# A two-layer decoder trunk: loads taken in turn, a written order for the first projection, and squares of the norm on ScalarE

## The chip, the cores and the metric

One core of one Trainium2 chip runs the whole kernel. The metric is the device time of one execution in microseconds; the time of a version is the median over its runs. The engines are TensorE (PE), VectorE (DVE), ScalarE (ACT), GpSimd (POOL) and SyncE (SP, which only issues loads and stores here).

## The reference

The input x has 512 tokens of 1024 channels, float32. Two layers follow one another, and each adds a mixer and a gated feed-forward part to x:

```
for layer in range(2):
    h = rms_norm(x, norm_mix[layer])
    x = x + (even_mixer(h, ...) if layer == 0 else odd_mixer(h, ...))
    h = rms_norm(x, norm_ffn[layer])
    x = x + (silu(h @ w_gate) * (h @ w_up)) @ w_down        # 1024 -> 2816 -> 1024
rms_norm(x, g) = x * rsqrt(mean(x * x, -1) + 1e-6) * g
```

The mixer of layer 0 is stick-breaking attention (8 heads of 64) beside a gated convolution over three tokens (512 channels), from one input projection and into one output projection. The mixer of layer 1 picks, for each query, the 128 keys with the largest score of a small indexer, and does softmax attention over them (16 query heads, 4 key heads, norms on queries and keys, a bias that depends on distance).

## The kernel before, in words

The residual x lives transposed on the chip, as eight chunks of 128 channels by 512 tokens (`xT`). A float32 product is made of three products in a rounded format: each operand is split into a high half (ScalarE: `wh`, `hr`) and a low half (VectorE: `wl`, `lr`, the operand less its high half), and `mm3` (L104 to L106) adds high by high, high by low and low by high into one PSUM bank. A product of 128 by 512 stands for one of these three. A weight tile is loaded by SP into one of three raw buffers (`raw`, L146) and split into one of three pairs (`wh` L149, `wl` L150); a tile is needed every eight slots. A slot is one call of `slot()`, made after each three products: `after(n, f)` runs f n slots later, and so sets where f's instructions stand in the order that is traced. Where the text says slot n, it counts from the end of a projection.

Outside of `manual_schedule` a scheduler orders each engine's instructions by its own model; inside it, TensorE, VectorE, ScalarE and GpSimd follow the order that was traced. Before the change this covers only the mixer of layer 1 (up to the start of its feed-forward part).

The head. x comes in token-major and is turned into chunks by TensorE with the identity (L382), two chunks per load; ScalarE makes the high half times the norm's gain (L174) and a kept copy of the chunk (L385), VectorE the low half (L175). The turns go through two `z` banks. The rsqrt of the norm isn't applied to h but to results: the query products start on x times gain. They go into four banks (L104 to L106), and `first_rstd` makes the tokens' sums of squares on VectorE (L396), the rsqrt on ScalarE and a Newton step, and spreads the result over the partitions with `dg` (L409) and a product with ones (L411) into `rbc`. `stack` empties the four banks (copies L420, low halves L424), and the key products, again L104 to L106, take the first bank that comes free. Ahead of it all stand 24 warm-up products of ones (L331, two instructions each).

The norms behind a projection. `residual_proj` adds each result of a projection to `xT` (L657, or L654 and L655 where rbc scales it), splits the new chunk (L174, L175) for the next projection, and adds its square into `ssq`: GpSimd squares and adds (L268, L272, L273), and for the last chunk ScalarE squares (L275) and VectorE adds (L276). `rstd_mm` runs some slots into the next projection (6 behind layer 0's mixer and layer 1's mixer, 7 behind layer 0's feed-forward part): the product with ones (L289), L291, a table load and rsqrt on ScalarE (L292), three Newton instructions (L281 to L283). Eight slots later `rstd_cols` (L300, L302) makes the same values one per token. The evacuations of the next projection wait for rbc.

Of the kernel before, what the change touches and what calls it, by code (L numbers as in the profile page):

```python
# [8 lines left out]
F32 = mybir.dt.float32  # L9
F32R = mybir.dt.float32r  # L10
ALU = mybir.AluOpType
AF = mybir.ActivationFunctionType
# [3 lines left out]
P = 128  # L16
S = 512
D = 1024
# [3 lines left out]
HC = HID // P  # L22
WARM = 24
ORDER = None
RATE0, LAG0 = 0.8, 5
LAGR_FFN, LAGR_MIX = 5, 7
L1_ORDER = {mybir.EngineType.PE, mybir.EngineType.DVE, mybir.EngineType.Activation,
            mybir.EngineType.Pool}
LAG_W, LAG_KI, LAG_DOT, LAG_CH, LAG_TK, LAG_TQ, LAG_T1, LAG_N, LAG_C, LAG_LO, LAG_P, EXPS = 3, 8, 5, 4, 8, 6, 4, 8, 11, 2, 3, 1
LAG_Z = 14  # L30
# [10 lines left out]
TAKEN = -3.4e38  # L41
ARENA_KB = 104.5

EARLY = 2
# [9 lines left out]
LAG_TK = 8  # L54
LAGR_FFN = 6
LAG_KLO = 1
# [19 lines left out]
class Net:  # L76
# [65 lines left out]

    def new_weights(self, src, kk, n, lo):
        nc = self.nc
        raw = self.wraw.tile([P, kk, n], F32, name="raw", tag="raw")
        nc.sync.dma_start(raw, src)  # L146
        wh = self.wsp.tile([P, kk, n], F32R, name="wh", tag="wh")
        wl = self.wsp.tile([P, kk, n], F32R, name="wl", tag="wl")
        nc.scalar.copy(wh, raw)  # L149
        (lo or nc.vector).tensor_tensor(wl, raw, wh.bitcast(F32), op=ALU.subtract)  # L150
        return wh, wl
# [111 lines left out]

    def stats_add(self, c):

        nc = self.nc
        if c == 0:
            nc.gpsimd.tensor_tensor(self.ssq, self.xT[:, c], self.xT[:, c], op=ALU.mult)  # L268
            return
        sq = self.cst.tile([P, S], F32, name="sqx", tag="sqx")  # L270
        if c < KC - 1:
            nc.gpsimd.tensor_tensor(sq, self.xT[:, c], self.xT[:, c], op=ALU.mult)  # L272
            nc.gpsimd.tensor_tensor(self.ssq, self.ssq, sq, op=ALU.add)  # L273
        else:
            nc.scalar.activation(sq, self.xT[:, c], AF.Square)  # L275
            nc.vector.tensor_tensor(self.ssq, self.ssq, sq, op=ALU.add)  # L276

# [6 lines left out]

    def rstd_mm(self):

        nc = self.nc
        ps = self.bank("z", "pstat")
        nc.tensor.matmul(ps, self.ones, self.ssq, start=True, stop=True)  # L289
        v = self.cst.tile([P, S], F32, name="sqx", tag="sqx")  # L290
        nc.vector.tensor_scalar(v, ps, 1.0 / D, EPS, op0=ALU.mult, op1=ALU.add)  # L291
        nc.scalar.activation(self.rbc, v, AF.Abs_reciprocal_sqrt)  # L292
        self.newton(self.rbc, v, self.ssq)
        self.after(8, self.rstd_cols)

# [9 lines left out]
    def setup(self):  # L305
# [20 lines left out]
        self.cols = cst.tile([P, 48], F32, name="cols")  # L326
        nc.scalar.dma_start(rows, I["norm_mix"].rearrange("l (c p) -> (l c) p", p=P))

        warm = self.bank("z", "pstat")
# [6 lines left out]
    def setup_rest(self):  # L336
        nc, I = self.nc, self.I
        rows = self.rows2
        nc.scalar.dma_start(rows[0:16, :], I["norm_ffn"].rearrange("l (c p) -> (l c) p", p=P))
        nc.scalar.dma_start(rows[16:28, :], I["ev_conv_w"][0].rearrange("w (c p) -> (w c) p", p=P))  # L340
# [30 lines left out]

    def load_x(self, xp):

        nc = self.nc
        xr = self.I["x"].rearrange("o (b p) d -> p (o b) d", p=P)
        xt = xp.tile([P, TB, D], F32, name="x_tm")
        for i in range(4):
            nc.sync.dma_start(xt[:, :, i * 256:(i + 1) * 256], xr[:, :, i * 256:(i + 1) * 256])
            for c in (2 * i, 2 * i + 1):
                ps = self.bank("z", "pstat")  # L380
                for tb in range(TB):
                    nc.tensor.transpose(ps[:, tb * P:(tb + 1) * P], xt[:, tb, c * P:(c + 1) * P],  # L382
                                        self.ident)
                self.split(self.xh3(c), ps, g=self.g_mix(0, c))
                nc.scalar.copy(self.xT[:, c], ps)  # L385
            self.x_tm = xt
            yield

    def first_rstd(self, xp):
# [14 lines left out]
        nc.vector.tensor_scalar(self.rq[:, TB:], self.rcol, 0.125, None, op0=ALU.mult)  # L404
        dg = xp.tile([P, S], F32, name="dg")
        ps = self.bank("z", "pstat")
        for tb in range(TB):
            t = slice(tb * P, (tb + 1) * P)
            nc.vector.tensor_scalar(dg[:, t], self.ident, self.rcol[:, tb:tb + 1], None,  # L409
                                    op0=ALU.mult)  # L410
            nc.tensor.matmul(ps[:, t], self.ones, dg[:, t], start=True, stop=True)  # L411
# [121 lines left out]
    def layer0_mix(self):  # L533
# [8 lines left out]
        with self.tc.tile_pool(name="xin", bufs=1) as xp:  # L542

            loads = self.load_x(xp)
            ps = [self.acc() for _ in range(4)]
            next(loads)
            for k0 in range(0, KC, 2):
                next(loads, None)
                wh, wl = self.weights(W[k0 * P:(k0 + 2) * P, 0:512].rearrange(
                    "(k p) n -> p k n", p=P), 2, 512)  # L550
                for m in range(4):
                    c = slice(m * P, (m + 1) * P)
                    for k in range(2):
                        h, l = xs[k0 + k]
                        self.mm3(ps[m], wh[:, k, c], wl[:, k, c], h, l, k0 + k == 0,
                                 k0 + k == KC - 1)
            self.first_rstd(xp)
            for m in range(4):
                qs = self.R(32 + 4 * m, 2, S)
                self.stack([(qs[0][:, e], qs[1][:, e]) for e in range(2)], ps[m])  # L560
                heads.append(qs[0])
        self.setup_rest()
# [6 lines left out]
        with self.tc.tile_pool(name="l0", bufs=1) as sp:  # L569
# [67 lines left out]
            for j in range(4):  # L637
# [5 lines left out]
            self.residual_proj(I["ev_w_out"][0], att + conv, self.xh3,  # L643
                               lambda c: self.g_ffn(0, c), pair=2)

    def residual_proj(self, W, ins, out3, gain, scale_r=False, tmp=None, pair=1, part=False,
                      lo=None):

        nc = self.nc

        def ev(m, ps):
# [4 lines left out]
            else:  # L656
                nc.vector.tensor_tensor(self.xT[:, m], self.xT[:, m], ps, op=ALU.add)  # L657
            if not part:
                self.split(out3(m), self.xT[:, m], g=gain(m))
                self.stats_add(m)  # L660
        self.proj_fm(W, 0, D, ins, ev, pair=pair, lo=lo)
        if not part:
            self.after(LAGR_MIX if scale_r else LAGR_FFN, self.rstd_mm)


    def ffn(self, layer, xs, g0):
# [5 lines left out]
        with self.tc.tile_pool(name=f"ffn{layer}", bufs=2) as fp:  # L672
# [30 lines left out]
            if not last:  # L703
                self.plan(self.fm_tiles(Wd, 0, D, HC, 256, 4, 1, None) + self.l1_tiles())
                self.residual_proj(Wd, gs, self.xh3, lambda c: self.g_mix(1, c), scale_r=True,
                                   tmp=fp)
                return
# [23 lines left out]
    def layer1_mix(self):  # L731
# [15 lines left out]
        with ExitStack() as es:  # L747
# [328 lines left out]
            while self.slots < start + 4 * len(order) + LAG_C + LAG_P + 4:  # L1076
                self.slot()
            self.few_banks(None)
            self.residual_proj(Wo[512:1024], half[4:8], lambda c: out3[c],
                               lambda c: self.g_ffn(1, c))  # L1080
        self.ffn(1, [(o[0], o[2]) for o in out3], 0)
# [49 lines left out]
```

## Time and profile before

| what | value |
|---|---|
| median of 3 runs | 1233.53 us (1232.91 to 1233.72) |
| the profiled execution | 1230.06 us |
| its span, first to last instruction | 1228.3 us |
| mean granted clock of TensorE | 0.996 |
| busy: TensorE, VectorE, ScalarE, GpSimd | 97%, 55%, 38%, 15% |

The profiled execution is one of its own, 3.47 us under the median; its span leaves out 1.76 us around the first and the last instruction. Matmuls overlap, so a busy TensorE is read from the distance of starts and not from durations.

### The profile page before, as it was taken

The page shows a single profiled execution, that of the slowest core. Times are in us where ns is not written, and L with a number is a line of the kernel's source. Part 1 is how long each engine was busy: PE and PEld are TensorE (multiplying, and loading weights), DVE is VectorE, ACT ScalarE, POOL GpSimd, SP SyncE. Part 2 cuts the span into 40 slices and gives each one's busy share as a digit, 9 for nine tenths or more (in the row PEclk, how much of TensorE's full clock was granted, in tenths as well). Part 3 has the DMA queues.
Part 4 walks back from the last instruction along what each step waited for, and adds up shares of the span by engine and source line. Part 5 has one row for each costly group of instructions (what it writes and reads, how often), then busy time and mean ns, then how long its engine had stood idle before and what let it go on. Part 6 is the DMA issues. An engine that isn't in the chain of part 4 may idle for free.

```text
span 1228.3 us, 14473 instructions
## 1 busy us (share of the span) xinstructions
PE 1196.7 (97%) x5573; PEld 982.4 (80%) x5573; DVE 669.5 (55%) x1064; ACT 466.2 (38%) x755; POOL 189.3 (15%) x228
## 2 busy tenths in 40 slices
PE   9999999999999999999999889998999999999998
PEld 8787878788888888888787678887888888888886
DVE  6769965634343343444589988757444444342322
ACT  5656733332233222222263379654322222322120
POOL 1334303200000000122135444226000000000000
PEclk9999999999999999999999999999999999999999
DMA  6231223333333332232223221112333233323330
GB/s 206 68 91 53 60 79 97 92 94 95 103 86 103 92 97 94 95 95 87 86 89 93 77 70 35 53 50 88 86 88 101 87 103 86 103 90 99 111 112 35
DMA packets 103637, 108.32 MB, mean 88 GB/s; under 512 B 4660, under 2 KB 89696, under 8 KB 103568
## 3 DMA queue, kind: packets, MB, share of 16 engines
q1 hardware_dynamic: 102768, 106.21, 29.0%
q10 hardware_dynamic: 800, 1.18, 0.3%
q8 instruction: 44, 0.72, 0.2%
q14 instruction: 25, 0.20, 0.1%
HBM read 105.24 MB, written 2.14 MB: 87 GB/s over the span
## 4 chain that ended last, share of the span: by engine, by line
PE 79%; DVE 12%; issue 5%; ACT 2%; POOL 2%; DMA 1%; ACTq 0%; POOLq 0%; DVEq 0%
PE acc L104 20%; PE acc L106 20%; PE acc L105 20%; PE acc L220 4%; PE acc L219 4%; PE acc L221 4%; DVE wl L150 2%; DVE w L825 1%; DVE L L828 1%; PE pt L1009 1%; DVE arena L175 1%; DVE om L458 1%; DVE xT L657 1%; PE z L433 1%; PE po L105 1%
## 5 line engine op out<-in xcount | busy, mean ns | idle before, releaser
L104 PE MATMUL acc<-arena,wh 128*128 128x512 f32 (+2 forms) x1176 | 468.1, 398 | 1.4 <-DVE xT L657 1.0
L106 PE MATMUL acc<-arena,wl 128*128 128x512 f32 (+2 forms) x1176 | 459.8, 391 | 0.0
L105 PE MATMUL acc<-arena,wh 128*128 128x512 f32 (+2 forms) x1176 | 456.7, 388 | 1.4 <-DVE arena L175 1.3
L150 DVE TENSOR_TENSOR wl<-raw,wh 128x1024 fp32r<-128x1024 f32 (+1 forms) x175 | 220.8, 1262 | 347.3 <-ACT wh L149 347.2
L149 ACT CAST wh<-raw 128x1024 fp32r<-128x1024 f32 (+1 forms) x191 | 198.6, 1041 | 462.7 <-issue 196.5
L106 PEld LDWEIGHTS acc<-arena,wl 128*128 128x128 f32 (+1 forms) x1176 | 220.7, 188 | 50.3 <-issue 0.2
L105 PEld LDWEIGHTS acc<-arena,wh 128*128 128x128 f32 (+1 forms) x1176 | 221.1, 188 | 47.4 <-DVE arena L175 2.3
L104 PEld LDWEIGHTS acc<-arena,wh 128*128 128x128 f32 (+1 forms) x1176 | 221.1, 188 | 45.1 <-DVE xT L657 2.1
L219 PE MATMUL acc<-wh,arena 128*128 128x512 f32 x272 | 108.9, 400 | 0.3 <-DVE arena L175 0.3
L220 PE MATMUL acc<-wl,arena 128*128 128x512 f32 x272 | 108.2, 398 | 0.0
L221 PE MATMUL acc<-wh,arena 128*128 128x512 f32 x272 | 108.1, 397 | 0.0
L221 PEld LDWEIGHTS acc<-wh,arena 128*128 128x128 f32 x272 | 51.4, 189 | 12.2
L219 PEld LDWEIGHTS acc<-wh,arena 128*128 128x128 f32 x272 | 51.5, 189 | 12.1 <-DVE arena L175 0.7
L220 PEld LDWEIGHTS acc<-wl,arena 128*128 128x128 f32 x272 | 51.5, 189 | 11.5
L683 DVE TENSOR_TENSOR ft<-acc,rbc 128x512 f32<-128x512 f32 x44 | 30.5, 692 | 55.2 <-PE acc L106 55.0
L268 POOL TENSOR_TENSOR ssq<-xT 128x512 f32<-128x512 f32 x3 | 3.5, 1169 | 327.8 <-DVE xT L655 274.0
L150 POOL TENSOR_TENSOR wl<-raw,wh 128x1024 fp32r<-128x1024 f32 x16 | 38.9, 2430 | 69.3 <-ACT wh L149 67.8
L685 ACT ACTIVATE fs<-ft 128x512 f32<-128x512 f32 x44 | 27.5, 629 | 52.2 <-DVE ft L683 52.2
L690 DVE TENSOR_TENSOR fp<-acc,fs 128x512 f32<-128x512 f32 x44 | 30.4, 692 | 28.5 <-PE acc L106 28.5
L433 PE MATMUL z<-arena 128*128 128x384 f32 (+3 forms) x120 | 41.2, 346 | 4.8 <-DVE mx L976 2.8
L976 DVE CUSTOM_DVE_ANT_0 L<-z,bias 128x128 f32<-128x128 f32 (+3 forms) x64 | 30.7, 486 | 18.2 <-PE z L975 17.6
L986 ACT ACTIVATE L<-L,mx 128x128 f32<-128x128 f32 (+3 forms) x64 | 35.8, 560 | 11.9 <-DVE sm L993 9.4
(205 smaller groups left out, 1285.9 us busy)
## 6 DMA issues: line engine op xcount, KB each, us to landing
raw<-in_ffn_w_gate_dram SPq DMA_DIRECT2D x44, 512.0 KB, 3.8
raw<-in_ffn_w_up_dram SPq DMA_DIRECT2D x44, 512.0 KB, 3.7
raw<-in_ffn_w_down_dram SPq DMA_DIRECT2D x42, 512.0 KB, 3.7
raw<-in_ev_w_in_dram SPq DMA_DIRECT2D x24, 512.0 KB, 3.9
raw<-in_od_w_in_dram SPq DMA_DIRECT2D x16, 512.0 KB, 3.5
raw<-in_ev_w_out_dram SPq DMA_DIRECT2D x8, 512.0 KB, 3.4
bias<-F SPq DMA_DIRECT2D x16, 256.0 KB, 3.2
raw<-in_od_w_out_dram SPq DMA_DIRECT2D x8, 512.0 KB, 3.4
```

The costliest lines, as they stand in the source:

```text
L104: mm(ps, wh, xh, start=first, stop=False)
L105: mm(ps, wh, xl, start=False, stop=False)
L106: mm(ps, wl, xh, start=False, stop=last)
L149: nc.scalar.copy(wh, raw)
L150: (lo or nc.vector).tensor_tensor(wl, raw, wh.bitcast(F32), op=ALU.subtract)
L219: mm(ps[tb], h[:, t], wh[:, k], start=c == 0, stop=False)
L220: mm(ps[tb], h[:, t], wl[:, k], start=False, stop=False)
L221: mm(ps[tb], l[:, t], wh[:, k], start=False, stop=c == kc - 1)
L433: self.nc.tensor.matmul(z, qs, kd, start=True, stop=False)
L683: nc.vector.tensor_tensor(t, ps, self.rbc, op=ALU.mult)
L976: nc.vector.tensor_tensor_reduce(out=u["ls"][:, r], in0=z, in1=bias[h][:, 0:nk][:, ::-1], scale=1.0, scalar=FILL, op0=ALU.add, op1=ALU.max ...
L986: nc.scalar.activation(ls[:, r], ls[:, r], AF.Exp, bias=mx[:, r:r + 1], accum_out=sm[:, r:r + 1])
```

## The change

Five things are changed.

1. x is loaded in five spans (128, 128, 256, 256 and 256 channels), and each of the first three is followed by the load of the query weights of the same channels. The products of the query go through these spans, under `manual_schedule`: the turns and splits of two chunks stand in the order ahead of the products of the chunks before them, and the kept copies right behind. 15 warm-up products are left, and a small ScalarE activation early in the setup draws its table load forward.
2. The token norms stay in that fixed order: the four reductions come behind the last weight split, then the stacks, then the product with ones.
3. The small loads of `setup_rest` wait, through a copy of `rcol`, until the token norms are there.
4. All squares behind a projection are made by ScalarE, into two buffers in turn where rbc isn't in use; GpSimd keeps the sum for all but the last chunk. Where rbc doesn't scale the result, the last chunk's square and sum come before its split.
5. The sums matmul comes at slot 8, 9 and 11 in place of 6, 7 and 6 (after the mixer of layer 0, after its feed-forward part, after the mixer of layer 1); behind the mixer of layer 0 there is no `rstd_cols`. The indexer's key in layer 1 is emptied two slots later.

```diff
-WARM = 24
+WARM = 15
-LAGR_FFN, LAGR_MIX = 5, 7
+LAGR_FFN, LAGR_MIX = 5, 9
-LAG_W, LAG_KI, ... = 3, 8, ...
+LAG_W, LAG_KI, ... = 3, 10, ...
+X_SPANS = ((0, 1), (1, 2), (2, 4), (4, 6), (6, 8))
-LAGR_FFN = 6
+LAGR_FFN = 8
...
-    def stats_add(self, c):
+    def stats_add(self, c, free):
         if c == 0:
-            nc.gpsimd.tensor_tensor(self.ssq, self.xT[:, c], self.xT[:, c], op=ALU.mult)
+            nc.scalar.activation(self.ssq, self.xT[:, c], AF.Square)
             return
-        sq = self.cst.tile([P, S], F32, name="sqx", tag="sqx")
-        if c < KC - 1:
-            nc.gpsimd.tensor_tensor(sq, self.xT[:, c], self.xT[:, c], op=ALU.mult)
-            nc.gpsimd.tensor_tensor(self.ssq, self.ssq, sq, op=ALU.add)
-        else:
-            nc.scalar.activation(sq, self.xT[:, c], AF.Square)
-            nc.vector.tensor_tensor(self.ssq, self.ssq, sq, op=ALU.add)
+        sq = (self.rbc if free and c % 2 else
+              self.cst.tile([P, S], F32, name="sqx", tag="sqx"))
+        nc.scalar.activation(sq, self.xT[:, c], AF.Square)
+        (nc.gpsimd if c < KC - 1 else nc.vector).tensor_tensor(self.ssq, self.ssq, sq, op=ALU.add)
...
-        self.after(8, self.rstd_cols)
+        if cols:
+            self.after(8, self.rstd_cols)
...
+        nc.scalar.activation(self.rcol[:, 0:1], self.zero, AF.Copy, scale=self.ones[:, 0:1])
...
+        nc.vector.tensor_copy(rows, self.rcol[0:32, 0:1].to_broadcast([32, P]))
         nc.scalar.dma_start(rows[0:16, :], I["norm_ffn"].rearrange("l (c p) -> (l c) p", p=P))
...
+    def load_x(self, xp, W):
+        xr = self.I["x"].rearrange("o (b p) d -> p (o b) d", p=P)
+        self.x_tm = xp.tile([P, TB, D], F32, name="x_tm")
+        raws = []
+        for i, (a, b) in enumerate(X_SPANS):
+            c = slice(a * P, b * P)
+            nc.sync.dma_start(self.x_tm[:, :, c], xr[:, :, c])
+            if i < 3:
+                raws.append(self.load_raw(W[c, 0:512].rearrange("(k p) n -> p k n", p=P),
+                                          b - a, 512))
+        return raws
+
+    def turn_x(self, c):
+        ps = self.bank("z", "pstat")
+        for tb in range(TB):
+            nc.tensor.transpose(ps[:, tb * P:(tb + 1) * P],
+                                self.x_tm[:, tb, c * P:(c + 1) * P], self.ident)
+        self.split(self.xh3(c), ps, g=self.g_mix(0, c))
+        return lambda: nc.scalar.copy(self.xT[:, c], ps)
+
+    def queries(self, W, raws):
...
+        keep = self.turn_x(0)
+        halves(0)
+        keep1 = self.turn_x(1)
+        keep()
+        halves(1)
+        keep1()
+        for i in range(5):
+            dot(i, (0, 1))
+            n = 2 + 2 * i
+            if n < KC:
+                keep = self.turn_x(n)
+            dot(i, (2, 3))
+            if n < KC:
+                keep1 = self.turn_x(n + 1)
+                keep()
+                halves(i + 2)
+                keep1()
...
+            raws = self.load_x(xp, W)
+            with self.tc.manual_schedule(engines=L1_ORDER):
+                self.queries(W, raws)
+                dg = self.first_rstd(xp)
                 for m in range(4):
-                qs = self.R(32 + 4 * m, 2, S)
-                self.stack([(qs[0][:, e], qs[1][:, e]) for e in range(2)], ps[m])
-                heads.append(qs[0])
+                    qs = self.R(32 + 4 * m, 2, S)
+                    self.stack([(qs[0][:, e], qs[1][:, e]) for e in range(2)], self.qps[m])
+                    heads.append(qs[0])
+                self.first_rbc(dg)
...
             if not part:
+                first = m == KC - 1 and not scale_r
+                if first:
+                    self.stats_add(m, not scale_r)
                 self.split(out3(m), self.xT[:, m], g=gain(m))
-                self.stats_add(m)
+                if not first:
+                    self.stats_add(m, not scale_r)
         self.proj_fm(W, 0, D, ins, ev, pair=pair, lo=lo)
         if not part:
-            self.after(LAGR_MIX if scale_r else LAGR_FFN, self.rstd_mm)
+            self.after(lagr, lambda: self.rstd_mm(cols))
```

Here `halves(i)` splits the weights of span i and `dot(i, ms)` makes its products into the banks ms. `lagr` is 8 by default and for layer 0's mixer, which also has `cols=False`; it is `LAGR_MIX` (9) behind layer 0's feed-forward part and 11 behind the mixer of layer 1.

## Rows read from the trace of the kernel before

**Rows 1.** The page, part 1: busy us, share of the span, instructions.

```profile
PE 1196.7 (97%) x5573; PEld 982.4 (80%) x5573; DVE 669.5 (55%) x1064; ACT 466.2 (38%) x755; POOL 189.3 (15%) x228
```

**Rows 2.** Windows, a quiet stretch: length, busy us (instructions) by engine, clock, DMA.

```profile
175.00:200.00 25.00, 25.00 (x111) 20.52 (x110) 11.51 (x13) 6.47 (x7) 0.00 (x0) 1.00 0.27 87
```

**Rows 3.** Waits of TensorE over the span: total us, times, longest.

```profile
PE pstat L289 <- DVE ssq L276: 4.7, 3, 3.7
```

**Rows 4.** Timeline of TensorE, head: start, us, operation, idle before it.

```profile
9.24 1.09 PE L382 MATMUL pstat<-eye,x_tm 128*128 128x128 f32 x8
...
10.67 0.51 PE L104 MATMUL acc<-arena,wh 128*128 128x512 f32 x1 [0.34 <-ACT arena L174]
...
36.46 1.05 PE L411 MATMUL pstat<-dg,ones 128*128 128x128 f32 x8
...
37.61 0.50 PE L104 MATMUL acc<-arena,wh 128*128 128x512 f32 x1
```

**Rows 5.** Windows of TensorE alone over the warm-up: busy, clock, DMA.

```profile
1.12:5.12 4.00, 4.00 (x19) 1.00 0.79 247
...
6.12:9.08 2.96, 2.96 (x28) 1.00 0.89 304
```

**Rows 6.** Chain that ended last, head: the turn of two chunks.

```profile
24.75 0.87 PE pstat L382 x8
```

**Rows 7.** Groups by line and tile: durations in ns (min/median/max), or busy us, mean ns.

```profile
L174 ACT ACTIVATE arena<-pstat,cols 128x512 fp32r<-128x512 f32 x8 | 5.2, 684 | 0.3 <-PE pstat L382 0.3
...
L385 ACT COPY xT<-pstat 128x512 f32<-128x512 f32 x8 | 4.5, 585 | 1.2 <-DVE arena L175 1.1
...
L149 ACT CAST wh<-raw x191: 622/1054/1082, 9.0 to 1207.5; 128x1024 fp32r<-128x1024 f32 x186, 128x512 fp32r<-128x512 f32 x4, 128x576 fp32r<-128x576 f32 x1
L150 DVE TENSOR_TENSOR wl<-raw,wh x175: 692/1226/2316, 10.0 to 1208.6; 128x1024 fp32r<-128x1024 f32 x170, 128x512 fp32r<-128x512 f32 x4, 128x576 fp32r<-128x576 f32 x1
...
L396 DVE CUSTOM_DVE_ANT_0 junk<-x_tm x4: 1215/1218/1227, 14.0 to 23.0; 128x1024 f32<-128x1024 f32 x4
```

**Rows 8.** Line L175, low halves of x, by source: ns min/median/max.

```profile
L175 DVE SCALAR_TENSOR_TENSOR arena<-xT,cols,arena x24: 740/1482/1782, 201.9 to 856.5; 128x512 fp32r<-128x512 f32 x24
L175 DVE SCALAR_TENSOR_TENSOR arena<-pstat,cols,arena x8: 740/745/750, 11.2 to 27.5; 128x512 fp32r<-128x512 f32 x8
```

**Rows 9.** Timeline of VectorE, head.

```profile
28.36 0.16 DVE L281 TENSOR_TENSOR t<-rcol 128x4 f32<-128x4 f32 x1
...
29.10 0.87 DVE L409 TENSOR_SCALAR dg<-eye,rcol 128x128 f32<-128x128 f32 x4
...
33.74 4.22 DVE L424 TENSOR_TENSOR arena<-acc,arena 64x512 fp32r<-64x512 f32 x6 [0.45 <-ACT arena L420]
```

**Rows 10.** Timeline of ScalarE, head: the first weight cast.

```profile
8.95 1.05 ACT L149 CAST wh<-raw 128x1024 fp32r<-128x1024 f32 x1 [3.78 <-DMA raw<-in_ev_w_in_dram]
```

**Rows 11.** Timeline of TensorE behind layer 1's mixer.

```profile
857.90 1.13 PE L289 MATMUL pstat<-ssq,ones 128*128 128x512 f32 x2 [3.72 <-DVE ssq L276]
```

**Rows 12.** Timeline of TensorE at the start of layer 1.

```profile
601.70 0.46 PE L105 MATMUL acc<-arena,wh 128*72 128x512 f32 x1 [1.32 <-DVE arena L175]
...
602.96 1.55 PE L289 MATMUL pstat<-ssq,ones 128*128 128x512 f32 x2 [0.58 <-DVE ssq L276]
```

**Rows 13.** Timeline of TensorE around L300, behind layer 0's mixer.

```profile
242.07 0.40 PE L106 MATMUL acc<-arena,wl 128*128 128x512 f32 x1
...
243.72 0.40 PE L105 MATMUL acc<-arena,wh 128*128 128x512 f32 x1
```

**Rows 14.** Windows behind the waits at the start of layer 1.

```profile
603.00:607.00 4.00, 4.00 (x10) 2.67 (x11) 1.72 (x3) 1.62 (x3) 0.00 (x0) 0.57 0.00 1
```

**Rows 15.** Timeline of ScalarE at the start of layer 1.

```profile
601.12 0.63 ACT L275 ACTIVATE sqx<-xT 128x512 f32<-128x512 f32 x1 [2.45 <-POOL ssq L273]
```

**Rows 16.** Timeline of VectorE at the start of layer 1.

```profile
607.39 0.69 DVE L283 SCALAR_TENSOR_TENSOR rbc<-ssq,rbc 128x512 f32<-128x512 f32 x1
```

**Rows 17.** Windows in the mixer of layer 0.

```profile
100.00:125.00 25.00, 22.43 (x117) 18.43 (x116) 23.85 (x38) 15.97 (x32) 9.14 (x29) 1.00 0.23 64
```

## What is expected of the change, and why

> **What bounds the kernel now.** I read the page first, then the waits of TensorE, then the timeline around each of those waits. The page has TensorE busy for 97% of the span [rows 1], and in a quiet stretch it starts a 128x512 product every 0.227 us (25.00 us over 110) with no idle time at all [rows 2]. So a microsecond is won only where TensorE waits, or where it is given work that it needn't do. Of the 1228.3 us it is idle for 31.6 (less 1196.7 busy). The largest group is the sums matmul of the norm (L289): 4.7 us in three goes [rows 3]. The other place is the head, where the query products begin at 10.67 us and the first sums of the token norms (L411) follow at 36.46 us [rows 4]; those 25.8 us hold 96 products, 21.8 us at 0.227, and the turns of x.
>
> **The head.** Three things set when the query products start. The warm-up holds TensorE until 9.08: its 48 instructions (two for each of 24 matmuls) run at about 0.21 us each at first, 19 of them in 4.0 us, and at about 0.11 us later, 28 in 2.96 us [rows 5]. The clock column reads 1.00 over both, so in this stretch the pace shows the level and the column doesn't. Nine matmuls fewer are 18 instructions at the later pace: 2.0 us. The first turn, at 9.24 [rows 4], then comes at 7.24. A chunk's turn costs 0.44 us of TensorE (0.87 for two) [rows 6].
>
> Now the order written out by hand. ScalarE must do in turn: high half of chunk 0 (0.68; its turn is done at 7.8, half of the 1.09 us of two turns [rows 4] after 7.24), high half of its weights (a half-size cast, 0.62), high half of chunk 1 (0.68), kept copy of chunk 0 (0.59), weights 1, kept copy 1 [rows 7]. The first product can so start at 7.8 + 0.68 + 0.62, about 9.2, which is 1.5 us earlier than before. VectorE follows with the low half of x (0.745, [rows 8]) and of the weights (0.69, [rows 7]), so the third product has to wait until 10.1. The turns of chunks 2 and 3 need the two z banks, that is the kept copies at 10.4 and 11.6. By hand that puts the end of the first chunk's 12 products and of the turns 0 to 3 at 13.3. From there on TensorE has 84 products (19.1) and 4 turns (1.8): 34.2, against 36.46. The gain at L411 is 2.3 us.
>
> What comes behind it is the cost of the fixed order. The token norms read all of x, in 4 reductions of 1.22 us [rows 7]; with the short instructions between them I take 5.2 us. Before, the scheduler put them into gaps; now they stand on VectorE behind the last weight split. That split comes after the turn of chunk 7, 11 us before the end of the products: at 23.2, then 0.68, 0.59 and 1.05 on ScalarE and 1.23 on VectorE, done at 26.8. Reductions end at 32.0; the rsqrt, the Newton steps and dg take about 2.0 more (1.6 of it from the first Newton step at 28.36 to the end of dg at 29.97) [rows 9]; dg is ready at 34.0, as TensorE gets there. Behind dg the first stack empties a bank with two subtractions of 0.70 [rows 9]: 35.4. The keys need that bank. TensorE fills 1.0 us of it with L411. So the keys start near 35.5, against 37.61 [rows 4]: **2.1 us** gained. Upper bound: with no wait at all behind the first turn the products end at 7.24 + 21.8 + 3.5 = 32.5 and the keys start 1.15 later, 3.9 us gained. Lower bound: TensorE is idle for about 1.5 us between 8 and 10 us, and idle time has cost the clock at 600 us (below, 1.7 us); with that and 1.2 us more on VectorE 0.8 us are lost. I take 2.1, nearest to the rows' own chain.
>
> The five x loads and three weight loads are issued together. Small loads of other constants move behind the token norms; their only readers here are the convolution and the norm gains, tens of us later. The x data is no bound: the turn of chunk 0 followed the warm-up at once. The weights were: ScalarE's first cast waited for them until 8.95 [rows 10]. They were loaded behind two x loads, 1 MB; now they stand behind a quarter of that and are half as large, so I take them to be there by 8.5, when the cast is due; if not, each microsecond is lost in full, up to the 2.1. The early table load is 1.28 us of ScalarE before any data is there, at no cost.
>
> **The sums matmul after layer 0's mixer (8 slots instead of 6).** The wait before L289 goes: of the 4.7 us [rows 3] the two other places have 3.72 and 0.58 [rows 11, 12], so here it is 0.4. Two slots of three products are 1.4 us. In place of rstd_cols nothing is done here: from the product at 242.07 to the second one behind it at 243.72 are 1.65 us, where two pitches are 0.46 us, so it cost **1.2 us** [rows 13]. Together **1.6 us**. The later rstd stalls no one: the first evacuation that needs it is at slot 12, and TensorE wants its bank back at slot 33, some 14 us later.
>
> **The same in layer 1's last projection (11 slots).** The wait is 3.72 us [rows 11]; it began after six slots, and five more slots are 3.4 us of products that are there to be done. Even with no faster sum only 0.3 us would be left, and the squares are faster now. I put 0.2 us against it, since the second weight tile is now asked for while VectorE still works off the last chunk: **3.5 us**. Bounds 2.5 and 3.7.
>
> **Into layer 1 (9 slots instead of 7).** Here TensorE waits twice: 1.32 us for the low half of chunk 6, then 0.58 us for the sum [rows 12]. Behind that the granted clock is 0.57 over 603 to 607 us: 4.0 x 0.43 = 1.7 us lost after those pauses [rows 14]. 3.6 us in all. ScalarE's square of the last chunk waited 2.45 us for GpSimd, which did square and sum [rows 15]; with the squares on ScalarE (0.63 each, [rows 15]) GpSimd keeps only the sum. The split of x on VectorE, which held up TensorE, takes a median of 1.48 us beside GpSimd and 0.74 at least; from PSUM it is 0.745 at the median [rows 8]. With a faster split the low half comes 1.0 to 1.3 us sooner. 0.3 us of new or left waits: **3.3 us**. Lower bound 1.3 (the pauses shrink, the clock still falls). L300 moves with the sum, eight slots behind it; before, rbc took from 602.96 to 608.07 [rows 12, 16], 5.1 us, and eight slots of three products with 384 columns (three quarters of 0.227 each) are 4.1, and L289 itself adds some 0.8, so 0.2 us may be lost there, which is in the 0.3.
>
> The Trainium skill (SBUF — State Buffer, "SBUF: two separate sides") says that GpSimd and a VectorE instruction with two SBUF inputs take one pair of ports as an exclusive lock, for the whole instruction. The doubled split agrees with it. By that rule the sum that stays on GpSimd could still block a split that comes behind it, and the 1.3 us of the first wait would come back in part; by the rows as summed above they don't.
>
> Twenty-one more squares on ScalarE are 7 per stage, 0.63 us each, against one chunk in 2.7 us: split 0.7, square 0.63 and half a cast, hidden.
>
> **Sum.** 2.1 + 1.6 + 3.3 + 3.5 = 10.5 us. The profiled execution took 1230.06 us, 1.76 over its span; less 10.5 it would be 1219.6. The median of the runs is 3.47 above the profiled one, so the forecast is 1233.5 - 10.5 = **1223.0 us**.
>
> **Rivals.** *The head gives nothing* (2.1 lost to the fixed order or to a drop of the clock in the 1.5 us of early pauses): 8.4 us are left, 1225.1 us. For it: VectorE's chain of 5.2 + 2.0 + 1.4 us lands just when TensorE needs it. Against: TensorE still starts 1.5 us sooner.
>
> *VectorE swallows what is gained.* Between 100 and 125 us VectorE is busy for 23.85 of 25 us [rows 17]. If such stretches end when VectorE's own work is done, what TensorE gains before them is lost in them: the head's 2.1 and layer 1's 3.3 go, 1228.4 us is left. Against it: VectorE's work there starts from TensorE's products, so it moves with them.
>
> *Slower: the clock stays low in the head.* With 15 warm-up matmuls TensorE has done 30 of the 48 instructions, and the pace rose only after about 24 of them [rows 5]. If it falls back at the pauses at 8 to 10 us and stays at 1.2 GHz, each product costs 0.227 us more. It eats the 10.5 us after 46 of the 96 products and is slower by over 0.2% from 57 on; with all 96 the time is 1245 us. Against: the warm-up still ends after the rise. The Trainium skill (TensorE: Matmul & The Clock Gate, Part 1) says that the slow rate is the default and that work releases it; by that rule less work before a pause is a risk, and the trace agrees in that the warm-up began slowly.
>
> **How the numbers follow.** Forecast 0.55, its own range 1219.5 to 1225; no gain in the head 0.23; VectorE swallows it 0.10; clock 0.05; what I haven't thought of 0.07. 0.2% is 2.5 us, about what a measurement can tell here. Faster: 0.55 + 0.23 + 0.08 + 0.02 = 0.88. Same: 0.02 + 0.03 = 0.05. Slower: 0.05 + 0.02 = 0.07. The low end adds the head's upper bound (1.8 more), layer 1's 0.3 and 0.2 left and some 2 us of shorter splits: 1218.5. The high end takes in the second rival: 1229.5.
>
> **What would show it.** First product near 9.2 us, L411 near 34.2, keys near 35.5; no wait over 0.3 us before L289 in all three places; no L300 in the first of them; a clock of 1.00 behind the second; splits of x near 0.75 us at the median. It would be wrong if TensorE waits for the bank of the keys by over 2 us, if L300 waits for rbc, or if TensorE's pace in the head is 0.45 us a product.

## The result, and the profile after

| what | before | after |
|---|---|---|
| median of 4 runs, us | 1233.22 (1232.34 to 1233.72) | 1223.99 (1222.72 to 1224.40) |
| ratio to before | | 0.9924, 95% interval 0.9907 to 0.9941 |
| profiled execution, us | 1230.06 | 1224.39 |
| its span, us | 1228.3 | 1222.5 |
| mean granted clock of the profiled execution | 0.996 | 0.995 |

The change made the kernel 9.2 us faster at the median; 1223.0 was forecast. The two profiled executions are only 5.7 us apart, which matters below. In the after kernel the lines of the helpers have moved: the turn is L399, `mm3` L105 to L107, the reductions L451, `dg` L462, the product with ones L471, `stack`'s low halves L484, the split of x L181 and L182, the sums matmul L293 and the output's last addition L766.

The waits of TensorE, those that have come in or changed (total us, times, longest). The 4.7 us in front of the sums matmul [rows 3] have no successor: L293 isn't in the list at all. The first line is new and was in no step of the prediction.

```profile
PE acc L226 <- DVE fo L766: 2.0, 1, 2.0
...
PE pstat L471 <- DVE dg L462: 1.0, 1, 1.0
...
PE acc L105 <- DVE arena L484: 0.9, 1, 0.9
PE acc L105 <- ACT wh L156: 0.8, 1, 0.8
...
PE acc L106 <- DVE arena L182: 0.6, 1, 0.6
```

The timeline of TensorE in the head, beside [rows 4]:

```profile
8.98 0.50 PE L105 MATMUL acc<-arena,wh 128*128 128x512 f32 x1 [0.85 <-ACT wh L156]
...
34.06 0.40 PE L107 MATMUL acc<-arena,wl 128*128 128x512 f32 x1
35.47 1.13 PE L471 MATMUL pstat<-dg,ones 128*128 128x128 f32 x8 [1.01 <-DVE dg L462]
37.48 0.47 PE L105 MATMUL acc<-arena,wh 128*128 128x512 f32 x1 [0.88 <-DVE arena L484]
```

The query products begin at 8.98 and end with the one at 34.06, close to the forecast (9.2, 34.2). Then TensorE stands still twice, and the keys start at 37.48 where 37.61 was before. The timeline of VectorE, beside [rows 9], tells why:

```profile
25.64 1.23 DVE L157 TENSOR_TENSOR wl<-raw,wh 128x1024 fp32r<-128x1024 f32 x1 [0.67 <-ACT wh L156]
26.78 1.22 DVE L451 CUSTOM_DVE_ANT_0 junk<-x_tm 128x1024 f32<-128x1024 f32 x1
...
27.92 1.22 DVE L157 TENSOR_TENSOR wl<-raw,wh 128x1024 fp32r<-128x1024 f32 x1
29.06 1.22 DVE L451 CUSTOM_DVE_ANT_0 junk<-x_tm 128x1024 f32<-128x1024 f32 x1
...
30.20 1.22 DVE L157 TENSOR_TENSOR wl<-raw,wh 128x1024 fp32r<-128x1024 f32 x1
31.34 1.22 DVE L451 CUSTOM_DVE_ANT_0 junk<-x_tm 128x1024 f32<-128x1024 f32 x1
...
32.60 1.23 DVE L451 CUSTOM_DVE_ANT_0 junk<-x_tm 128x1024 f32<-128x1024 f32 x1
...
35.05 0.87 DVE L462 TENSOR_SCALAR dg<-eye,rcol 128x128 f32<-128x128 f32 x4
35.95 5.66 DVE L484 TENSOR_TENSOR arena<-acc,arena 64x512 fp32r<-64x512 f32 x8
```

The last weight split of the queries ends at 26.8, as forecast. But two weight splits of the next projection (27.92 and 30.20) stand among the four reductions, 2.3 us in all, and `dg` is done at 35.9, not 34.0.

The three sums matmuls in the timeline of TensorE, beside [rows 11 to 13]: none of them waits, and in front of the second only one pause is left, of 0.63 us.

```profile
235.92 1.02 PE L293 MATMUL pstat<-ssq,ones 128*128 128x512 f32 x2
...
599.08 0.45 PE L106 MATMUL acc<-arena,wh 128*72 128x512 f32 x1 [0.63 <-DVE arena L182]
...
600.80 1.02 PE L293 MATMUL pstat<-ssq,ones 128*128 128x512 f32 x2
...
853.70 1.02 PE L293 MATMUL pstat<-ssq,ones 128*128 128x512 f32 x2
```

The window behind the second (clock, the third column from the right, 1.00; 0.57 in [rows 14]), and the low halves of x, whose median behind a projection fell from 1482 [rows 8] to 748 ns:

```profile
601.00:605.00 4.00, 4.00 (x22) 3.53 (x21) 2.37 (x4) 1.57 (x2) 0.00 (x0) 1.00 0.00 0
```
```profile
L182 DVE SCALAR_TENSOR_TENSOR arena<-xT,cols,arena x24: 737/748/1784, 201.9 to 851.1; 128x512 fp32r<-128x512 f32 x24
```

The median hides the two low halves that matter, those of the last chunks into layer 1, which TensorE waits for. They are no faster than before. What comes sooner is a product of 128 by 1 (`gk`) ahead of them on VectorE. The timelines of VectorE, before and then after:

```profile
597.94 0.88 DVE L760 TENSOR_TENSOR gk<-cols 128x1 f32<-128x1 f32 x1
...
599.88 2.42 DVE L175 SCALAR_TENSOR_TENSOR arena<-xT,cols,arena 128x512 fp32r<-128x512 f32 x2
```
```profile
596.02 0.16 DVE L815 TENSOR_TENSOR gk<-cols 128x1 f32<-128x1 f32 x1
...
597.24 2.45 DVE L182 SCALAR_TENSOR_TENSOR arena<-xT,cols,arena 128x512 fp32r<-128x512 f32 x2
```

At the output the new wait. First TensorE, then VectorE, which waits for a store that still holds its `fo` buffer, then the DMA issues from 1150 to 1162 us (KB each, median us to landing) with the one packet of 16 KB that loads instructions:

```profile
1159.81 0.50 PE L226 MATMUL acc<-wh,extra 128*128 128x512 f32 x1 [2.01 <-DVE fo L766]
```
```profile
1159.01 1.41 DVE L766 SCALAR_TENSOR_TENSOR fo<-acc,rcol,xT 128x512 f32<-128x512 f32 x2 [5.89 <-DMA out_dram<-fo]
```
```profile
q8 instruction: 1, 0.02, 0.5%
...
out_dram<-fo ACTq DMA_DIRECT2D x2, 256.0 KB, 6.4
out_dram<-fo SPq DMA_DIRECT2D x2, 256.0 KB, 6.3
```

The last number of a line is a median over those issues alone whose landing the profile has; here that is the first of the two on each queue. The profile of the kernel before has no landing of its first two stores. The 144 packets, 256 KB together, that its queue q10 moved for the first one (issued at 1160.27) all begin between 1160.2 and 1164.2 us, so it took near 4 us; the two stores behind them landed in 2.1 us. No instruction load falls between 1158 and 1170 us there. In head_only (an experiment below) the first two stores landed in 4.3 and 4.2 us with no load among them; the first of them:

```profile
out_dram<-fo ACTq DMA_DIRECT2D x1, 256.0 KB, 4.3
```

The account, from the starts of the same product in the two profiled executions (the n-th product of one against the n-th of the other, the difference read on both sides of each place):

| place | forecast, us gained | measured |
|---|---|---|
| head, up to the first key product | 2.1 | 0.1 |
| sums behind layer 0's mixer, with `rstd_cols` | 1.6 | 1.8 |
| into layer 1 | 3.3 | 3.2, of which 0.6 is lost again by 632 us |
| layer 1's last projection | 3.5 | 4.0 |
| between 632 and 830 us | 0 | -0.7 |
| output stores | 0 | -2.1 |
| sum | 10.5 | 5.7 |

Single executions differ by parts of this. Between 632 and 830 us nothing was changed, and yet against before the products there lose 0.7 us in after, 0.4 in sums_only and 2.2 in fo4, and nothing in early_norms. After has the low clock for longer there (0.53 granted over 671 to 678 us; before 1.00 over these and 0.58 over 678 to 682).

### The profile page after: what moved, and what is told of

It reads as the page before. It is cut to its first block, busy times and chain, and to the rows that moved or that the text cites. A ratio compares the mean times of both kernels' runs of the same rounds, so it can differ in the third digit from the quotient of the medians.

```text
span 1222.5 us, 14432 instructions
## 1 busy us (share of the span) xinstructions
PE 1192.4 (98%) x5547; PEld 978.9 (80%) x5547; DVE 649.9 (53%) x1065; ACT 476.9 (39%) x778; POOL 157.2 (13%) x207
## 4 chain that ended last, share of the span: by engine, by line
PE 81%; DVE 11%; issue 4%; POOL 2%; ACT 2%; DMA 1%; POOLq 0%; DVEq 0%; ACTq 0%
PE acc L105 21%; PE acc L107 21%; PE acc L106 20%; PE acc L226 4%; PE acc L227 4%; PE acc L228 4%; DVE w L880 1%; DVE L L883 1%; PE pt L1064 1%; DVE wl L157 1%; DVE om L518 1%; PE z L493 1%; DMA out_dram<-fo 1%; PE po L106 1%; DVE ssq L883 1%
## 5 line engine op out<-in xcount | busy, mean ns | idle before, releaser
L105 PE MATMUL acc<-arena,wh 128*128 128x512 f32 (+2 forms) x1176 | 465.5, 396 | 2.8 <-DVE xT L708 1.0
L107 PE MATMUL acc<-arena,wl 128*128 128x512 f32 (+2 forms) x1176 | 459.5, 391 | 0.1
L157 DVE TENSOR_TENSOR wl<-raw,wh 128x1024 fp32r<-128x1024 f32 (+1 forms) x176 | 212.8, 1209 | 356.6 <-ACT wh L156 356.5
L105 PEld LDWEIGHTS acc<-arena,wh 128*128 128x128 f32 (+1 forms) x1176 | 220.7, 188 | 48.0 <-DVE xT L708 2.1
L107 PEld LDWEIGHTS acc<-arena,wl 128*128 128x128 f32 (+1 forms) x1176 | 220.5, 187 | 48.2 <-DVE wl L157 0.4
L280 POOL TENSOR_TENSOR ssq<-ssq,sqx 128x512 f32<-128x512 f32 x12 | 18.6, 1548 | 375.1 <-ACT sqx L279 375.1
L178 ACT CAST arena<-fp 128x512 fp32r<-128x512 f32 x36 | 22.2, 616 | 46.9 <-DVE fp L745 46.9
```

Of the source, the lines that this page charges most:

```text
L105: mm(ps, wh, xh, start=first, stop=False)
L107: mm(ps, wl, xh, start=False, stop=last)
```

## The experiments

Each time stands beside runs of the kernel before on the same chip.

**The two halves apart.** One kernel has only the sums (squares on ScalarE, later slots, no `rstd_cols` in the first place), the other only the head (loads in turn, written order, 15 warm-ups).

```diff
 # sums_only: load_x, first_rstd, WARM as before; stats_add, residual_proj, slots as after
 # head_only: the other way round
```

> The kernel before with only the squares on ScalarE, the later sums matmul and no rstd_cols behind the first mixer; the head is as before. If the head gave nothing net (the trace after has it level with before at 68 us), this keeps the whole gain: about 1224 us, 9 us under before, and in the trace 1.8 us at the first sums matmul, 2.5 at the second and 4 at the third. If the head gave the 2.1 us of the forecast and the trace after misleads, it is about 1226 us.

> The kernel before with only the new loads, the fixed order of the query products and 15 warm-up matmuls; squares, slots and rstd_cols are as before. If VectorE's chain (reductions with weight splits between them, dg, first stack) swallows the head's gain: query products end near 34.1 us, keys start near 37.5, time within 0.2% of before (1232 to 1234). If the head gives the 2.1 us that were forecast: about 1231, keys near 35.5.

Measured: sums_only 1223.08 us, ratio 0.9932 (0.9918 to 0.9946). head_only 1230.78 us, ratio 0.9992 (0.9982 to 1.0003): no gain that can be measured. Its first key product comes 0.05 us later than before. So nearly all of the change is the sums. How far one execution of a head can be trusted is seen from kernels that share it. With the head of before, the keys start at 37.61 us in before, 37.85 in squares_only and 38.4 in sums_only and slots_only; with the head of after, at 37.48 in after and 38.19 in fo4. A difference of under some 0.8 us in the head isn't told by one trace; the 2 us that are missing are more than that.

head_only shows one thing more. Its wait at the third sums matmul is the one of before (3.71 us), but here the clock falls behind it; in the profiled execution of before it didn't (1.00 over 857.9 to 861.9). First its timeline, then its window:

```profile
858.03 1.12 PE L296 MATMUL pstat<-ssq,ones 128*128 128x512 f32 x2 [3.71 <-DVE ssq L283]
```
```profile
859.00:863.00 4.00, 4.00 (x12) 3.14 (x11) 3.01 (x4) 1.68 (x2) 0.00 (x0) 0.57 0.23 80
```

**The sums' two parts apart.** slots_only has the later slots and nothing else, squares_only the squares on ScalarE and the last square ahead of its split.

```diff
 # slots_only: before, with
-LAGR_FFN, LAGR_MIX = 5, 7        # third place 6
+LAGR_FFN, LAGR_MIX = 5, 9        # first place 8, third place 11; LAG_KI 8 -> 10
 # squares_only: before, with stats_add(c, free) of the change and its place ahead of the split
```

> The kernel before with only the sums matmul's later slots (8, 9, 11) and the indexer key two slots later; the squares stay on GpSimd and rstd_cols stays in all places. Theory 1, the products put ahead of the sums matmul make the gain: no wait of TensorE before the sums matmul in all three places (4.7 us before), the low halves of x still 1.48 us at the median, the wait of 1.32 us for the low half of chunk 6 stays and the granted clock still falls behind it. 4.2 to 4.7 us less than before, ratio about 0.9963. Theory 2, the squares on ScalarE make it: a wait of 2 us or more stays in front of the third sums matmul and the gain is under 2.5 us.

> The kernel before with only the squares on ScalarE and the last chunk's square ahead of its split; old slots (6, 7, 6), rstd_cols stays. Theory 1, the later slots make the gain at the third sums matmul: its wait of 3.72 us shrinks by 1 to 1.5 us at most (the last square and sum no longer stand behind the split and GpSimd's backlog), while the low halves of x fall to 0.75 us and the 1.32 us wait into layer 1 to about 0.6: 2 to 4 us less than before, ratio 0.997 to 0.998. Theory 2, the squares make it: the third wait falls under 1.5 us, both waits into layer 1 go with the fall of the clock, 6 us less, ratio 0.995. The two single parts, added, should give the 7.7 us or so of the sums alone, less the 1.2 of rstd_cols; if they add to more, they remove the same wait twice.

Measured: slots_only 1225.45 us, 0.9952 (0.9938 to 0.9965); squares_only 1224.34 us, 0.9946 (0.9933 to 0.9959). Gains place by place, by the same products:

| place | slots_only | squares_only | after |
|---|---|---|---|
| layer 0's mixer | 0.6 | 0.7 | 1.8, with 1.2 for `rstd_cols` |
| into layer 1 | 2.4, 0.6 lost again | 2.3 | 3.2, 0.6 lost again |
| layer 1's last projection | 3.4 | 3.8 | 4.0 |

Either part alone takes away nearly all of the 4.7 us in front of the sums matmul (0.29 us is left in slots_only, 0.58 in squares_only): they remove the same waits. The timelines of TensorE, slots_only first:

```profile
601.76 0.45 PE L105 MATMUL acc<-arena,wh 128*72 128x512 f32 x1 [1.32 <-DVE arena L175]
...
856.05 1.13 PE L289 MATMUL pstat<-ssq,ones 128*128 128x512 f32 x2 [0.29 <-DVE ssq L276]
```
```profile
600.46 0.46 PE L105 MATMUL acc<-arena,wh 128*72 128x512 f32 x1 [0.63 <-DVE arena L175]
...
601.72 1.12 PE L286 MATMUL pstat<-ssq,ones 128*128 128x512 f32 x2 [0.58 <-DVE ssq L273]
...
852.44 1.12 PE L286 MATMUL pstat<-ssq,ones 128*128 128x512 f32 x2
```

slots_only keeps the pause of 1.32 us into layer 1 and leaves 0.29 us at the third sums matmul, as the prediction worked out for slots without faster squares; that is theory 1 of its expectation, but for the clock, which didn't fall. squares_only, at the old slot, waits for nothing there. That is against theory 1, which gave the squares 1 to 1.5 us of the 3.72, and as theory 2 has it, though the pauses into layer 1 stay. The timelines of VectorE around the last chunk's addition and the sum, before and then squares_only, take the wait apart:

```profile
854.29 0.68 DVE L657 TENSOR_TENSOR xT<-xT,acc 128x512 f32<-128x512 f32 x1
...
857.16 0.68 DVE L276 TENSOR_TENSOR ssq<-ssq,sqx 128x512 f32<-128x512 f32 x1
```
```profile
850.18 0.68 DVE L654 TENSOR_TENSOR xT<-xT,acc 128x512 f32<-128x512 f32 x1
...
851.69 0.69 DVE L273 TENSOR_TENSOR ssq<-ssq,rbc 128x512 f32<-128x512 f32 x1 [0.83 <-ACT rbc L272]
```

Before, TensorE comes to the sums matmul at 854.18 (3.72 us ahead of 857.90), and the addition begins 0.1 us after that; in squares_only it begins 2.3 us ahead of the matmul (852.44). These 2.4 us are VectorE's backlog: between 846 and 857 us of before, beside GpSimd, its weight splits take 1.7 us and all low halves but the last 1.4 to 1.5, in squares_only 1.2 and 0.75. From the start of the addition to the end of the sum it is 3.55 us before and 2.2 in squares_only. These 1.35 us are theory 1's: the sum no longer stands behind a weight split and a low half. For GpSimd itself nothing waited at the end: its last sum was done at 855.5, ScalarE's last square at 856.2. In both kernels the clock no longer falls behind the pauses of layer 1; the windows, slots_only and then squares_only:

```profile
603.00:607.00 4.00, 4.00 (x22) 3.52 (x21) 1.70 (x3) 1.70 (x3) 0.00 (x0) 1.00 0.01 3
```
```profile
603.00:607.00 4.00, 4.00 (x24) 3.73 (x22) 3.23 (x5) 1.57 (x2) 0.00 (x0) 1.00 0.00 0
```

Before, the two pauses were 1.32 and 0.58 us. In these executions dropping the second, or halving the first, was each enough: among the twelve traces the clock falls at this place only in the two that have both pauses in full, before and head_only (0.57 over 603 to 607 us in both). The 0.6 us lost again by 632 us occurs in slots_only, in sums_only and after, and not in squares_only: it belongs to the later slots (rstd 9, indexer key 10), behind which a z bank comes free late (a pause of 0.16 us and slower starts around it at 612 us). Which of the two slots does it was not tried apart.

**The reductions earlier.** After, with two reductions behind the turns of chunks 4 and 5 and two behind those of chunks 6 and 7.

```diff
+            for tb in {1: (0, 1), 2: (2, 3)}.get(i, ()):
+                self.token_sum(tb)
...
 # first_rstd: its four reductions are taken out; token_sum makes one of them
```

> The changed kernel with the four token reductions moved up in the fixed order: two behind the second span's turns, two behind the third's. If the wait for dg (1.0 us) and the wait for the bank of the keys (0.9 us) are what ate the gain: no wait before the product with ones, keys near 35.3 us, and 2 us less than the changed kernel, about 1222. If VectorE's later stretches swallow whatever comes early: keys near 35.3 too, but the sums matmul behind the first mixer as late as in the changed kernel, and 1224.

Measured: 1221.15 us, ratio 0.9910 (0.9896 to 0.9924). Two weight splits still stand among VectorE's work, but only two reductions are left behind the last weight split of the queries, and both waits of the head are gone (timeline of TensorE):

```profile
33.99 1.05 PE L476 MATMUL pstat<-dg,ones 128*128 128x128 f32 x8
34.80 0.47 PE L105 MATMUL acc<-arena,wh 128*128 128x512 f32 x1
```

The keys start 2.8 us sooner than before. At 68 us 2.1 of it are left (where the other 0.7 went is open), and at 595 us all of these still are (besides 1.9 of the sums): VectorE's busy stretch from 100 to 125 us swallows nothing.

**More buffers at the output.** After, with four buffers of `fo`; then both edits together.

```diff
-                    o = fp.tile([P, S], F32, name="fo", tag="fo")
+                    o = fp.tile([P, S], F32, name="fo", tag="fo", bufs=4)
```

> The changed kernel with four buffers in place of two for the output tiles. If the 2.0 us that TensorE waited near the end come from stores that took 6.3 us with two buffers, and stores are that slow in each execution: no wait there and about 1222 us. If the slow stores were of that one profiled execution: stores of 2.1 us in this trace or no difference in time, about 1224.

> The kernel after with the reductions of the token norms moved up between the turns and with four buffers of fo at the output instead of one or two. If the 2 us before the output's last banks come from the slow store that holds fo, no wait for fo is left and the time is 1.5 to 2 us under the one with early reductions alone: about 0.9895 of the kernel before. Rival: the store's delay only moves to the last store, which ends the kernel, and nothing is gained (0.991).

Measured: fo4 1222.62 us, 0.9920 (0.9906 to 0.9934); early_fo4 1219.17 us, 0.9899 (0.9886 to 0.9913). In both the wait for `fo` is gone though the first two stores are still slow, 5.7 to 5.9 us. (The 2.1 us of the expectation is what later stores took, see above.) The DMA issues of early_fo4 from 1150 to 1162 us, then the first store of early_w4, the same kernel with a shorter warm-up (below), in which no load falls between 1150.2 and 1155.2 us, when its first two stores have landed:

```profile
q8 instruction: 1, 0.02, 0.5%
...
out_dram<-fo ACTq DMA_DIRECT2D x2, 256.0 KB, 5.8
```
```profile
out_dram<-fo ACTq DMA_DIRECT2D x1, 256.0 KB, 4.2
```

Between 1160 and 1171 us, where after loses 2.1 us against before, fo4 gains 0.2 and early_fo4 0.2. At the median the 2 us do not show for fo4 alone (its profiled execution had one more fall of the clock, granted mean 0.994), so its place is shown by the trace and its worth by the median is open. early_fo4 is the fastest version with 15 warm-ups, but its interval holds both of the values that were expected (0.9895 and 0.991), so it doesn't settle that worth either.

**The length of the warm-up.**

```diff
-WARM = 15
+WARM = 24      # warm24;  4 in warm4, and in early_w4 (early_fo4 with 4)
```

> The kernel after with 24 warm-up matmuls instead of 15. Theory 1, the head's end is set by VectorE's chain (last weight split, reductions, dg, first bank), and that chain starts from TensorE's turns: everything in the head comes 1.5 to 2 us later, first product near 10.7, first key product near 39, about 1.7 us slower than the kernel after, ratio to before 0.9938. Theory 2, the loads and ScalarE set it: first product and keys move by under 0.5 us and the time is that of the kernel after, 0.9924.

> The kernel after with 4 warm-up matmuls (8 instructions) instead of 15: a test of the slower rival, that too little work ahead of the head's pauses leaves TensorE at half its pace. If that rival has a place, the query products start 2 to 3 us sooner but run at about 0.45 us each for a part of the head, and the first key product comes at 37.5 us or later: no gain, or some us lost (each 10 products at half pace cost 2.3 us). If the pace of the head doesn't hang on the warm-up, first product near 6.5 us, keys near 35, about 2 us less than the kernel after (0.9908).

> The kernel with early reductions and four fo buffers, with 4 warm-up matmuls instead of 15. There TensorE has no wait left between the query products and the keys, so each us that the first product comes sooner, or is lost to a slower pace, should reach the end: with full pace 2 us less (about 0.988), with the slow pace over the first 10 to 20 products 0 to 3 us more (0.990 to 0.992).

Measured: warm24 1224.23 us, 0.9943 (0.9930 to 0.9955); warm4 1221.35, 0.9910 (0.9894 to 0.9927); early_w4 1218.99, 0.9892 (0.9878 to 0.9907). warm24: everything comes 1.5 us later than after, first product 10.50 and keys 39.02, so the chain that ends the head does begin at TensorE's turns. Its clock also falls behind the two pauses (timeline, then window):

```profile
37.01 1.13 PE L471 MATMUL pstat<-dg,ones 128*128 128x128 f32 x8 [1.02 <-DVE dg L462]
39.02 0.76 PE L105 MATMUL acc<-arena,wh 128*128 128x512 f32 x1 [0.88 <-DVE arena L484]
```
```profile
38.00:42.00 4.00, 3.12 (x9) 2.43 (x8) 3.87 (x7) 3.44 (x6) 0.00 (x0) 0.61 0.08 19
```

warm4: the first product starts at 7.72, but the first eight products and the turn among them go at half pace, mostly 0.43 us from one product to the next; from 12.07 on the distance is 0.23. The rows of its timeline on both sides, and the window around them, whose clock column reads 1.00:

```profile
9.57 0.63 PE L106 MATMUL acc<-arena,wh 128*128 128x512 f32 x1
10.00 0.63 PE L107 MATMUL acc<-arena,wl 128*128 128x512 f32 x1
...
12.30 0.40 PE L105 MATMUL acc<-arena,wh 128*128 128x512 f32 x1
12.54 0.39 PE L106 MATMUL acc<-arena,wh 128*128 128x512 f32 x1
```
```profile
8.00:12.00 4.00, 4.00 (x13) 3.22 (x12) 1.45 (x2) 2.65 (x5) 0.00 (x0) 1.00 1.08 374
```

Its keys start 0.3 us later than after's, within what single traces differ by. What it gains over after at the end isn't the head: its stores land in 4.4 us and nothing waits for them. early_w4, without those two waits in the head, ends 0.3 us ahead of early_fo4 in the trace, within what the measurement can tell; its interval decides between neither of the two expectations.

## Why the prediction was right, and where it wasn't

**The sums: right.** All three waits went, `rstd_cols` gave 1.2 us, the clock stayed at 1.00. The terms were 1.6, 3.3 and 3.5; measured are 1.8, 3.2 less 0.6, and 4.0. The new loss of 0.3 allowed for layer 1 is 0.6, and not where I looked for it (rbc) but at a z bank. The term for layer 1 has the right size by a wrong step. It was argued as a faster split; the two low halves there take 2.45 us after and 2.42 before, and the 0.7 us by which the pause shrinks are those of `gk` (0.88 to 0.16 us). slots_only shows that the slot alone does most of the term, since in its trace the second pause is gone and the clock doesn't fall.

**The lock.** In the after kernel the pause of 0.63 us into layer 1 is left, behind two low halves that take 2.45 us together from 597.24 while GpSimd adds from 596.74 to 598.48. The first of the two, begun beside GpSimd, takes 1.78 us, the second 0.74. The Trainium skill (SBUF — State Buffer, "SBUF: two separate sides") says that a VectorE instruction with two SBUF inputs and GpSimd exclude each other; the trace agrees, and so does `gk`, which has two such inputs: begun in the middle of GpSimd's square (597.45 to 598.81) it ends with it, at 598.82, and takes 0.88 us, and 0.16 without. So what the prediction set aside came true: the sum left on GpSimd blocks a split behind it, and about half of the 1.32 us came back.

**The head: the step that failed.** "Reductions end at 32.0 ... dg is ready at 34.0": they ended at 33.8 and 35.9. I costed VectorE's queue from the written order of the head alone; two weight splits of the keys stand in it as well. They take 1.14 us each by the distance of starts, and I had taken the reductions as one block. The first rival, in which the head gives nothing, came true in this place: 0.1 us. Early reductions brought the keys forward by 2.7 us against after (0.3 of it were there at the first product already), so the place of the reductions in the order was the cost, and TensorE's part of the head (9.2, 34.2) was sized rightly.

**The output: not thought of.** The profile has the landing of the first two stores in the eight kernels with the new head. In four of them (after, early_norms, fo4, early_fo4) the 16 KB instruction load falls while these stores are on their way, and they land in 5.7 to 6.4 us. In the other four (head_only, warm24, warm4, early_w4) it falls before or behind them, and they land in 4.1 to 4.4. early_fo4 and early_w4 differ in the warm-up alone, so the new head by itself doesn't make these stores slow. Only at 6.2 us and more, with the old buffers, does TensorE wait. That the load slows the store is argued from these eight traces; a kernel that moves nothing but the load was not tried.

**The other rivals.** VectorE swallows nothing in its busy stretch: early_norms carries its 2.1 us from 68 to 595 us. The slow pace in the head has no place with 15 warm-ups (0.23 us a product from 10.2 on) and a real one with 4. The Trainium skill (TensorE: Matmul & The Clock Gate, Part 1) has the slow rate as the default that work releases; warm4's 0.43 us a product agree.

**The number.** 1223.0 against 1223.99 is closer than the steps deserve; that is luck in part. In the profiled executions 5.7 us were gained, not 10.5. But I had carried the 3.47 us between before's profiled execution and its median over to the new kernel as a constant, and it is no constant: after's median is 0.4 us under its profiled execution. The 17 runs of before beside the first experiments have mean granted clocks of 0.992 to 0.996, about 0.994; those at 0.996 took 1230.3 to 1231.1 us, those at 0.992 1233.5 and 1235.4. Its profiled execution had 0.996, the top of them; the 4 of after have 0.995 to 0.997. Two thousandths of 1230 us are about 2.5 us, which is most of the 3.5. head_only's fall behind a wait of 3.71 us suggests how: such a wait costs the clock in one trace and not in another, and the change removed the wait. That this is what happens in the unprofiled runs of before is an inference from their clocks.

## What to carry to other kernels

Two remedies for one wait are to be priced together: here later slots and faster squares each removed nearly all of the same 4.7 us. Work taken off an engine that is not on the path can pay through its neighbour: with the squares off GpSimd, VectorE's splits beside it were shorter, and its last addition came 2.4 us sooner. When an order is fixed by hand, list everything that stands in the queue of the engine that ends the chain, the next stage's work too, and put what has its data early in front; the rewritten head gave nothing until the reductions were moved. A median over many instructions says nothing of the one that is waited for: the splits' median was halved, and the split that TensorE waits for stayed as long as it was. The distance of a profiled execution from the median can be the price of the waits themselves, so it shouldn't be added to the forecast of a kernel without them.

## What the runs showed of the hardware

The granted clock behind the same wait differs from trace to trace: 1.00 behind 3.72 us in before, 0.57 behind 3.71 us in head_only; 0.61 behind pauses of 1.02 and 0.88 us in warm24, 1.00 in after behind 1.01 and 0.88. In the first 12 us of warm4 the clock column reads 1.00 over products at 0.43 us each, so there the pace must be read from the starts. The output's first two 256 KB stores landed in 4.1 to 4.4 us in the four traces in which no instruction load of 16 KB fell among them, and in 5.7 to 6.4 us in the four in which one did. A VectorE product of 128 by 1 took 0.88 us beside a GpSimd instruction and 0.16 without, and a split of 128 by 512 took 1.78 and 0.74.
